# A decoder layer on one core: natural order in the first gate-and-up unit, sums placed behind the single block, two more weight sums made ahead

## The chip, the cores and the metric

The kernel runs on one core of a Trainium2 chip. The metric is the device time of one execution in microseconds (us), taken as the median of several runs; lower is better. The profile is of one execution of the same program.

## The reference

One decoder layer over 272 tokens (16 meta tokens in front of 256) of width 2048, in float32:

- s = s + 0.5 * FFN1(rms_norm(s)), where FFN(h) = (silu(h @ Wg) * (h @ Wu)) @ Wdown with a hidden width of 5632
- h = rms_norm(s); q, k, v, b, c, u = split(h @ w_in); a differential attention over q, k, v and a short gated convolution over b, c, u give two branches of width 1024
- each branch is multiplied by its w_branch, gated by sigmoid(h @ w_gate), and the two are added; s = s + merged @ w_out
- s = s + 0.5 * FFN2(rms_norm(s)), a last rms_norm, and the meta tokens are dropped

## The kernel before

Every matrix product is split into high and low parts: a tensor is cast to a high part (`wh` of the weights on ScalarE) and the rest is subtracted on VectorE (`wl`), and TensorE multiplies high by high, low by high and high by low. So each product of two blocks is three matmuls (lines 644 to 646 in the helper `product`).

The first FFN (`linear`, lines 360 to 439) multiplies plainly, weights stationary, 272 tokens wide. Most of what follows works on 256 tokens in `linear_mix` (line 622): a unit has an output of 2 x 512 columns (gate and up, or two gates) and runs over eight pairs of 128-row blocks of the weights. A pair is of one of three kinds, one letter each in a plan:

- D: the plain way, two tiles of two weight blocks, eight products, 24 matmuls of 128x512.
- S: Winograd's way with seven products, 21 matmuls. The weights are four tiles: a single block, two blocks, and two pairs of weight sums, t24 and t13. VectorE makes these sums on the spot in three operations (`sums`, lines 686 to 688).
- P: as S, but the weight sums were made ahead. In the first FFN a helper (`Making`, lines 316 to 339) loads quarters of such weights on POOL's DMA queue, VectorE adds them in three operations (lines 331 to 333), and POOL stores them to DRAM; `tick` starts a step of it every few chunks. A P pair loads three blocks and the two sums from there (lines 666, 673, 674), on the SP queue.

The activations have sums as well: `Mixed.sum_of_parts` (line 579) adds the parts of one pair, makes four sums of 128x128 blocks on VectorE (lines 589 to 592) and splits them (lines 614 and 615). Its temporaries carry the tag "sc", which has two buffers. The split of an S or P pair's single block takes two buffers of the same tag.

Products of one name are summed in one PSUM bank over the whole unit: D pairs feed 2, 3, 4 and x, S and P pairs feed 1 to 7. All eight banks are in use once a unit has seen both kinds, and x is complete with the last D pair; then `done` copies it out (line 736).

A unit's splits are issued ahead of its products: `step` holds the matmuls of up to three tiles back. Small work of other stages is spread through a unit by a list, `side`: one entry is taken when a pair's last tile is used. The entries of `out_done` (line 1234 on) turn the updated residual into the next operand h3: `turned(p)` transposes pair p on TensorE into a PSUM bank (line 1180), ScalarE and VectorE write its two parts (1184, 1185), and `sum_of_parts` follows. The order of the instructions on each engine comes from a scheduler that goes by this program order and by its own estimates of what is ready.

A plan holds the kinds, the pairs at which transposes of earlier results (`later`) are done, and a table that says behind which tile (pair, tile) which pair's weight sums are made. The plan of FFN2's first unit has a fifth entry, the order in which it goes through the pairs.

Of the kernel before, what the change touches and what calls it, by code (L numbers as in the profile page):

```python
# [15 lines left out]
P = 128  # L16
# [4 lines left out]
F = 5632  # L21
DC = D // P
GC = 4
GW = GC * P
# [17 lines left out]
LATER_AT = (4, 6)  # L42


GATES_FIRST = ("DDDSDSDS", (2,), {(2, 1): 3, (4, 1): 5, (6, 1): 7}, ())
GATES = ("PSDSDSDS", (), {(0, 3): 1, (2, 1): 3, (4, 1): 5, (6, 1): 7}, ())
Q = ("DSDSDSDS", (), {(0, 1): 1, (2, 1): 3, (4, 1): 5, (6, 1): 7}, ())
B_PLAN = ("DSDSDSDS", (2, 4), {(0, 1): 1, (2, 1): 3, (4, 1): 5, (6, 1): 7}, ())
FFN2_FIRST = ("DDPDPDPP", (1,), {}, (), (0, 1, 3, 4, 5, 2, 6, 7))
FFN2 = ("DDPPDSPP", (1,), {(4, 1): 5}, ())  # L50
FFN2_MORE = ("DPPPDSPP", (2,), {(4, 1): 5}, ())
OUT_FIRST = ("DDSDSDSD", (1,), {(1, 1): 2, (3, 1): 4, (5, 1): 6}, ())
OUT = ("DDDDSDSD", (), {(3, 1): 4, (5, 1): 6}, ())
DOWN_FIRST = ("DDDDSDSD", (1,), {(3, 1): 4, (5, 1): 6}, ())
DOWN = ("DDSDSDSD", (), {(1, 1): 2, (3, 1): 4, (5, 1): 6}, ())
DOWN_LAST = ("DDDSDS", (1,), {(2, 1): 3, (4, 1): 5}, ())
AHEAD = 3
W_LAST = 8 * GC
TICK_COUNT = 512
# [2 lines left out]
MORE_IN = (4, 5, 6, 7, 8, 9, 10)  # L62


def _made_in(plan):
    return [plan[4][i] if plan[4:] else i for i, kind in enumerate(plan[0]) if kind == "P"]


def _unit_plan(u):
    return FFN2_MORE if u in MORE_IN else FFN2 if u else FFN2_FIRST  # L70


GATE_UNITS = [GATES_FIRST] + [GATES] * (D // GW - 1)
MADE = [(0, d, p) for d, plan in enumerate(GATE_UNITS) for p in _made_in(plan)]
MADE += [(1, u, p) for u in range(F // GW) for p in _made_in(_unit_plan(u))]


@with_exitstack
def decoder_layer(ctx: ExitStack, tc: tile.TileContext, t, out):
    nc = tc.nc  # L80
# [5 lines left out]
    tmp = ctx.enter_context(tc.tile_pool(name="tmp", bufs=2))  # L86
# [46 lines left out]
    def load_vectors():  # L133
# [7 lines left out]
        out=mask[:, T - P :],  # L141
        in_=mask[:, T - P :],
# [152 lines left out]
    side = []  # L295
# [326 lines left out]
    def linear_mix(plan, a, w, name, done, k0=0, made=None, pairwise=False):  # L622

        kinds, turn_at, sums_at, by_load = plan[:4]
        at = plan[4] if plan[4:] else range(len(kinds))
        nd = kinds.count("D")
        ns = len(kinds) - nd
        left = {k: 2 * nd * (k in "234x") + ns * (k != "x") for k in "1234567x"}
        ps = {}

        def product(k, left_op, wh, wl):
            first = k not in ps
            if first:  # L640
                ps[k] = bank(name + k)
            left[k] -= 1
            hi, lo = left_op
            nc.tensor.matmul(ps[k], hi, wh, start=first, stop=False)  # L644
            nc.tensor.matmul(ps[k], lo, wh, start=False, stop=False)  # L645
            nc.tensor.matmul(ps[k], hi, wl, start=False, stop=left[k] == 0)  # L646
            if left[k] == 0:
                done(k, ps[k])

        def use(p, n, products):  # L650

            for k, left_op, wh, wl in products:
                product(k, left_op, wh, wl)
            if p in turn_at and later:
                later.pop(0)()
            if n == (1 if kinds[p] == "D" else 3):
                if p == 0:
                    flush()
                if side:
                    side.pop(0)()  # L660

        def load(p):

            st = wpool.tile([P, 4, GW], F32, tag="st", bufs=ST_BUFS, name="st")
            n = 3 if p in by_load or kinds[p] == "P" else 4
            nc.sync.dma_start(out=st[:, :n, :], in_=w[k0 // 2 + at[p], :, :n, :])
            if kinds[p] == "P":
                if pairwise:
                    t13s[p] = wpool.tile([P, 2, GW], F32, tag="tt", bufs=2, name="t13")
                else:  # L670
                    t13s[p] = aux.tile([P, 2, GW], F32, tag="act", name="t13")
                t24s[p] = wpool.tile([P, 2, GW], F32, tag="tt", bufs=2, name="t24")
                nc.sync.dma_start(out=t24s[p], in_=made[at[p]][:, 2:4, :])
                nc.sync.dma_start(out=t13s[p], in_=made[at[p]][:, 0:2, :])
            if kinds[p] == "S":
                if not by_load and (made is None or pairwise):
                    t13s[p] = wpool.tile([P, 2, GW], F32, tag="tt", bufs=2, name="t13")
                elif p not in by_load:
                    t13s[p] = aux.tile([P, 2, GW], F32, tag="act", name="t13")
                t24s[p] = wpool.tile([P, 2, GW], F32, tag="tt", bufs=2, name="t24")  # L680
            return st

        def sums(k):
            st, t13, t24 = loaded[k], t13s[k], t24s[k]
            if k not in by_load:
                nc.vector.tensor_add(t13, st[:, 1:3, :], st[:, 3:4, :].to_broadcast([P, 2, GW]))
            nc.vector.tensor_add(t24[:, 0, :], t13[:, 0, :], st[:, 2, :])
            last_sum[:] = [nc.vector.tensor_add(t24[:, 1, :], t24[:, 0, :], st[:, 0, :]).ins]  # L688

        t13s, t24s = {}, {}  # L690

        def prefetch(p):
            t13 = t13s[p] = aux.tile([P, 2, GW], F32, tag="act", name="t13")
            nc.gpsimd.dma_start(out=t13, in_=w[k0 // 2 + p, :, 1:3, :])
            nc.gpsimd.dma_start(out=t13, in_=w[k0 // 2 + p, :, 3:5, :], accum_op=ALU.add)

        far = 2 if by_load or (made is not None and not pairwise) else 1
        loaded = {k: load(k) for k in range(far)}
        for p, kind in enumerate(kinds):
            for k in by_load:  # L700
                if k == p + 4 or (p == 0 and k < 4):
                    prefetch(k)
            st = loaded[p]
            (a11, a21), (a12, a22) = ([a.block(2 * at[p] + c, i) for i in range(2)] for c in range(2))
            if kind == "D":
                tiles = [
                    (st[:, 1 - c :: 2, :], (("2", a1, 0), ("3", a1, 1), ("4", a2, 0), ("x", a2, 1)))
                    for c, (a1, a2) in enumerate(((a11, a21), (a12, a22)))
                ]
            else:  # L710
                s1, s2, s3, s4 = a.sums[at[p]]
                tiles = [
                    (st[:, 2:3, :], (("3", s4, 0),)),
                    (st[:, 0:2, :], (("1", a11, 1), ("2", a12, 0))),
                    (t24s[p], (("6", s2, 0), ("4", a22, 1))),
                    (t13s[p], (("5", s1, 0), ("7", s3, 1))),
                ]
            for n, (src, products) in enumerate(tiles):
                if n == 1 and p + far < len(kinds):
                    loaded[p + far] = load(p + far)  # L720
                wh, wl = parts(src, src.shape[1])
                if (p, n) in sums_at:

                    with tc.issue_after(part_last[1]):
                        sums(sums_at[p, n])
                products = [(k, left_op, wh[:, j, :], wl[:, j, :]) for k, left_op, j in products]
                step(lambda p=p, n=n, products=products: use(p, n, products), src.shape[1] > 1)
# [388 lines left out]
    for d in range(D // GW):  # L1116
# [28 lines left out]
        if d < 2:  # L1145
            n = 3 * d
# [93 lines left out]
    def out_done(u):  # L1240
        def f():
            if u == 0:
                side.append(lambda: None)
                for p in (0, 2):
                    side.append(lambda p=p: [turned(p), turned(p + 1), squares(0, 0, p // 2), squares(1, 0, p // 2)])
                side.append(lambda: [hn.sum_of_parts(2, tmp), hn.sum_of_parts(3)])
            else:
                side.extend(
                    (
                        lambda: [turned(4), squares(0, 1, 0), squares(1, 1, 0)],  # L1250
                        lambda: [turned(5), hn.sum_of_parts(5)],
                        lambda: [turned(6), squares(0, 1, 1), hn.sum_of_parts(6)],
                        lambda: [turned(7), squares(1, 1, 1)],
                        lambda: hn.sum_of_parts(7),
                        norm_tok,
                    )
                )

        return f
# [40 lines left out]
    for half in thirds:  # L1300
# [11 lines left out]
        for u in range(2):  # L1312
# [40 lines left out]
                )  # L1353
            elif u == 0:
                side.extend([lambda: None] * 2)
                side.extend(lambda p=p: ma.sum_of_parts(p) for p in (4, 6, 2))
                add_mix(DOWN_FIRST, ma, w_down, half[0] * GC, u, 0.5, "dma", lambda: None)
            elif not final:
                if half is thirds[0]:
# [90 lines left out]
```

## Time and profile before

| What | us |
|---|---|
| median of three runs | 2133.9 |
| lowest and highest of them | 2133.49 and 2135.06 |
| the profiled execution | 2133.6 |
| its span, first to last instruction | 2131.8 |
| TensorE busy | 2118.6 |
| VectorE busy | 1765.0 |
| ScalarE busy | 1138.7 |

The granted clock of TensorE is 0.999 of full speed over the span. Busy time is the union of an engine's instructions; matmuls overlap one another in the profile, so two of them that start 0.23 us apart each show 0.39 us. The stages follow one another as: first FFN (to some 770 us), k, q, b, v, c and u (to 1090), gates and branches (to 1350), out (to 1435), second FFN (to the end).

### The profile page before, as it was taken

Reading aid. Unit: us, or ns where it says so; the run is one execution under the profiler, and the core shown is the slowest. Engines: PE = TensorE matmul, PEld = TensorE weight load, DVE = VectorE, ACT = ScalarE, POOL = GpSimd, SP = SyncE. Lnnn points to the kernel's source line nnn. Section 1 sums busy time; section 2 is a strip of 40 time slices with the busy share of each in tenths; the row PEclk is TensorE's granted clock in tenths of the full one; section 3 lists DMA queues with packets and bytes.
Section 4 is the critical chain, followed back from the end, with each engine's and each line's share of the span. In section 5 each row is a group of like instructions: output and inputs, shape, how many; then the busy total and the mean of one; then the engine's idle time right before and its main releaser. Section 6 shows DMA issues by size and latency. Waiting matters only on the chain.

```text
span 2131.8 us, 33535 instructions
## 1 busy us (share of the span) xinstructions
PE 2118.6 (99%) x13096; PEld 1910.3 (90%) x13096; DVE 1765.0 (83%) x2458; ACT 1138.7 (53%) x1447; POOL 152.0 (7%) x241
## 2 busy tenths in 40 slices
PE   9999999999999999999999999999999999999998
PEld 9999999999999998899998888887888888888887
DVE  8777776677767878967888889998999999998997
ACT  6433343344443455645546655557665567656765
POOL 0111111111111110000000000000000100000000
PEclk9999999999999999999999999999999999999999
DMA  8989999999899875544455665566875988769863
GB/s 305 340 310 339 344 331 331 334 331 331 328 331 338 302 293 193 182 166 151 144 187 199 212 231 179 208 215 231 289 274 191 284 323 316 247 222 325 320 232 138
DMA packets 107007, 562.04 MB, mean 264 GB/s; under 512 B 12512, under 2 KB 12896, under 8 KB 66144
## 3 DMA queue, kind: packets, MB, share of 16 engines
q1 hardware_dynamic: 72720, 440.73, 57.6%
q0 software_dynamic: 33696, 118.50, 16.1%
q8 instruction: 102, 1.67, 0.3%
q10 hardware_dynamic: 432, 0.67, 0.1%
q14 instruction: 57, 0.47, 0.1%
HBM read 496.94 MB, written 58.72 MB: 261 GB/s over the span
## 4 chain that ended last, share of the span: by engine, by line
PE 99%; ACT 0%; DMA 0%; DVE 0%; issue 0%; SPq 0%; ACTq 0%
PE pg L644 6%; PE pg L645 6%; PE pg L646 6%; PE pd L427 4%; PE pd L425 4%; PE pu L425 4%; PE pu L426 4%; PE pu L427 4%; PE pd L426 4%; PE pg L425 4%; PE pg L427 4%; PE pg L426 4%; PE pd L644 4%; PE pd L646 4%; PE pd L645 4%; PE g L644 2%
## 5 line engine op out<-in xcount | busy, mean ns | idle before, releaser
L409 ACT CAST wh<-st 128x1024 fp32r<-128x1024 f32 x320 | 335.1, 1049 | 475.7 <-PE pu L426 143.2
L414 DVE TENSOR_TENSOR wl<-st,wh 128x1024 fp32r<-128x1024 f32 x320 | 390.3, 1223 | 217.9 <-ACT wh L409 217.7
L532 DVE TENSOR_TENSOR wl<-st,wh 128x1024 fp32r<-128x1024 f32 (+1 forms) x424 | 454.3, 1089 | 32.9 <-ACT wh L531 29.2
L531 ACT CAST wh<-st 128x1024 fp32r<-128x1024 f32 (+1 forms) x424 | 386.4, 945 | 153.6 <-PE pdx L645 27.7
L531 ACT CAST wh<-t 128x1024 fp32r<-128x1024 f32 x208 | 214.6, 1052 | 244.5 <-DVE t L688 184.0
L532 DVE TENSOR_TENSOR wl<-t,wh 128x1024 fp32r<-128x1024 f32 x208 | 248.2, 1221 | 58.8 <-ACT wh L531 54.4
L427 PE MATMUL pd<-mh,wl 128*128 128x272 f32 x704 | 203.1, 288 | 0.0
L425 PE MATMUL pg<-h,wh 128*128 128x272 f32 x704 | 201.9, 287 | 0.4 <-ACT wh L409 0.4
L425 PE MATMUL pd<-mh,wh 128*128 128x272 f32 x704 | 202.2, 287 | 0.0
L425 PE MATMUL pu<-h,wh 128*128 128x272 f32 x704 | 201.9, 287 | 0.0
L427 PE MATMUL pu<-h,wl 128*128 128x272 f32 x704 | 201.7, 287 | 0.0
L426 PE MATMUL pu<-h,wh 128*128 128x272 f32 x704 | 201.7, 286 | 0.0
L426 PE MATMUL pg<-h,wh 128*128 128x272 f32 x704 | 201.6, 287 | 0.0
L427 PE MATMUL pg<-h,wl 128*128 128x272 f32 x704 | 200.9, 287 | 0.0
L426 PE MATMUL pd<-ml,wh 128*128 128x272 f32 x704 | 200.8, 285 | 0.0
L645 PE MATMUL pg<-wh,h 128*128 128x512 f32 x373 | 146.1, 392 | 0.0
L644 PE MATMUL pg<-wh,h 128*128 128x512 f32 x373 | 145.5, 391 | 0.6 <-ACT h L1184 0.6
L646 PE MATMUL pg<-wl,h 128*128 128x512 f32 x373 | 145.4, 391 | 0.6 <-DVE wl L532 0.6
L426 PEld LDWEIGHTS pd<-ml,wh 128*128 128x128 f32 x704 | 133.5, 190 | 0.0
L425 PEld LDWEIGHTS pg<-h,wh 128*128 128x128 f32 x704 | 132.9, 189 | 0.7 <-ACT wh L409 0.7
L426 PEld LDWEIGHTS pg<-h,wh 128*128 128x128 f32 x704 | 132.8, 189 | 0.0
L426 PEld LDWEIGHTS pu<-h,wh 128*128 128x128 f32 x704 | 132.6, 188 | 0.0
(392 smaller groups left out, 5040.0 us busy)
## 6 DMA issues: line engine op xcount, KB each, us to landing
st<-in_ffn_w_gu_dram SPq DMA_DIRECT2D x121, 1024.0 KB, 7.4
st<-in_ffn_w_down_dram SPq DMA_DIRECT2D x82, 1024.0 KB, 7.1
mk<-in_ffn_made_of_dram POOLq DMA_DIRECT2D x108, 512.0 KB, 8.6
made<-mk POOLq DMA_DIRECT2D x108, 512.0 KB, 6.7
t<-made SPq DMA_DIRECT2D x108, 512.0 KB, 5.7
st<-in_ffn_w_gu_dram SPq DMA_DIRECT2D x51, 768.0 KB, 5.8
st<-in_w_in_dram SPq DMA_DIRECT2D x32, 1024.0 KB, 4.8
st<-in_w_gate_dram SPq DMA_DIRECT2D x29, 1024.0 KB, 4.8
```

The lines of the kernel that those rows point to most:

```text
L409: nc.scalar.copy(out=wh[:, :m, :], in_=sw)
L414: last_wl[:] = [nc.vector.tensor_sub(wl[:, :m, :], sw, wh[:, :m, :].bitcast(F32)).ins]
L425: nc.tensor.matmul(a, wh[:, i, f], act.part(c, 0, t0, t1), start=first, stop=False)
L426: nc.tensor.matmul(a, wh[:, i, f], act.part(c, 1, t0, t1), start=False, stop=False)
L427: nc.tensor.matmul(a, wl[:, i, f], act.part(c, 0, t0, t1), start=False, stop=last)
L531: part_last[:] = [nc.scalar.copy(out=wh, in_=src).ins]
L532: part_last.append(nc.vector.tensor_sub(wl, src, wh.bitcast(F32)).ins)
L644: nc.tensor.matmul(ps[k], hi, wh, start=first, stop=False)
L645: nc.tensor.matmul(ps[k], lo, wh, start=False, stop=False)
L646: nc.tensor.matmul(ps[k], hi, wl, start=False, stop=left[k] == 0)
```

## The change

1. FFN2's first unit goes through its pairs in natural order: D D D P D P P P over pairs 0 to 7, where it was pairs 0, 1, 3, 4, 5, 2, 6, 7 as D D P D P D P P. The kind of each pair stays. The code for such an order is removed.
2. In all plans the weight sums of an S pair are made behind the split of its own single block (place p, tile 0) and no longer behind the second tile of the plain pair before it (place p - 1, tile 1).
3. Two activation sums move in `side`: `hn.sum_of_parts(3)` three entries later in OUT's second unit, `ma.sum_of_parts(2)` two entries later in DOWN_FIRST.
4. In the first gate unit, places 1 and 3 become P pairs: D P D P D S D S for D D D S D S D S. The list of sums to be made ahead, MADE, grows from 54 to 56 pairs, and its makings (two halves a pair) from 108 to 112.

```diff
-GATES_FIRST = ("DDDSDSDS", (2,), {(2, 1): 3, (4, 1): 5, (6, 1): 7}, ())
-GATES = ("PSDSDSDS", (), {(0, 3): 1, (2, 1): 3, (4, 1): 5, (6, 1): 7}, ())
-Q = ("DSDSDSDS", (), {(0, 1): 1, (2, 1): 3, (4, 1): 5, (6, 1): 7}, ())
...
-FFN2_FIRST = ("DDPDPDPP", (1,), {}, (), (0, 1, 3, 4, 5, 2, 6, 7))
-FFN2 = ("DDPPDSPP", (1,), {(4, 1): 5}, ())
...
-OUT = ("DDDDSDSD", (), {(3, 1): 4, (5, 1): 6}, ())
+GATES_FIRST = ("DPDPDSDS", (2,), {(5, 0): 5, (7, 0): 7}, ())
+GATES = ("PSDSDSDS", (), {(0, 3): 1, (3, 0): 3, (5, 0): 5, (7, 0): 7}, ())
+Q = ("DSDSDSDS", (), {(1, 0): 1, (3, 0): 3, (5, 0): 5, (7, 0): 7}, ())
...
+FFN2_FIRST = ("DDDPDPPP", (1,), {}, ())
+FFN2 = ("DDPPDSPP", (1,), {(5, 0): 5}, ())
...
+OUT = ("DDDDSDSD", (), {(4, 0): 4, (6, 0): 6}, ())
...
-                side.append(lambda: [hn.sum_of_parts(2, tmp), hn.sum_of_parts(3)])
+                side.append(lambda: hn.sum_of_parts(2, tmp))
+                side.extend([lambda: None] * 2)
+                side.append(lambda: hn.sum_of_parts(3))
...
-                side.extend(lambda p=p: ma.sum_of_parts(p) for p in (4, 6, 2))
+                side.extend(lambda p=p: ma.sum_of_parts(p) for p in (4, 6))
+                side.extend([lambda: None] * 2)
+                side.append(lambda ma=ma: ma.sum_of_parts(2))
```

## Rows read from the trace of the kernel before

**Rows 1.** The page's first part: busy us, share of the span, instructions.
```profile
PE 2118.6 (99%) x13096; PEld 1910.3 (90%) x13096; DVE 1765.0 (83%) x2458; ACT 1138.7 (53%) x1447; POOL 152.0 (7%) x241
```

**Rows 2.** Windows: stretch, length, busy us (records) PE, PEld, DVE, ACT, POOL; clock; DMA share, GB/s.
```profile
50.00:750.00 700.00, 700.00 (x5668) 700.00 (x5667) 506.82 (x743) 282.45 (x318) 128.17 (x205) 1.00 0.90 330
...
1092.00:1142.00 50.00, 50.00 (x225) 41.37 (x224) 46.57 (x66) 31.05 (x40) 0.00 (x0) 1.00 0.57 194
...
1415.00:1435.00 20.00, 19.83 (x88) 16.07 (x87) 19.82 (x31) 10.36 (x13) 0.00 (x0) 1.00 0.59 198
1435.00:1460.00 25.00, 25.00 (x112) 19.80 (x111) 23.18 (x37) 18.05 (x29) 0.00 (x0) 1.00 0.77 270
1460.00:1486.00 26.00, 23.32 (x99) 16.76 (x98) 19.69 (x31) 17.12 (x22) 0.00 (x0) 1.00 0.62 211
1486.00:1506.00 20.00, 20.00 (x93) 16.60 (x93) 20.00 (x24) 13.38 (x16) 0.00 (x0) 1.00 0.72 257
1500.00:1526.00 26.00, 26.00 (x117) 21.52 (x116) 24.47 (x26) 18.77 (x22) 0.00 (x0) 1.00 0.84 286
```

**Rows 3.** Timeline of TensorE in the gates: start us, duration us, what.
```profile
1180.48 0.39 PE L644 MATMUL g<-wh,h 128*128 128x512 f32 x1
...
1181.16 0.39 PE L644 MATMUL g<-wh,h 128*128 128x512 f32 x1
```

**Rows 4.** Timeline of FFN2's first unit, its last three pairs.
```profile
1467.78 0.39 PE L646 MATMUL pgx<-wl,h 128*128 128x512 f32 x1
...
1468.92 0.58 ACT L736 COPY u2x<-pgx 128x512 f32<-128x512 f32 x1
...
1469.56 0.66 PE L1180 MATMUL h_ps<-ident,sT 128*128 128x128 f32 x4 [1.39 <-ACT u2x L736]
...
1475.27 0.63 ACT L531 CAST wh<-st 128x512 fp32r<-128x512 f32 x1
...
1476.66 0.68 DVE L532 TENSOR_TENSOR wl<-st,wh 128x512 fp32r<-128x512 f32 x1
...
1483.12 0.69 DVE L615 TENSOR_TENSOR sp<-sums,sp 128x512 fp32r<-128x512 f32 x1
```

**Rows 5.** Timeline of the first DOWN_FIRST at its second S pair.
```profile
1639.54 0.61 ACT L531 CAST wh<-st 128x512 fp32r<-128x512 f32 x1
1639.69 0.39 PE L645 MATMUL pd<-wh,m 128*128 128x512 f32 x1
...
1640.20 0.50 PE L644 MATMUL pd<-wh,sp 128*128 128x512 f32 x1
```

**Rows 6.** Timeline of a later gate unit at an S pair.
```profile
1244.10 0.69 DVE L532 TENSOR_TENSOR wl<-st,wh 128x512 fp32r<-128x512 f32 x1
...
1246.44 0.69 DVE L688 TENSOR_TENSOR t<-t,st 128x512 f32<-128x512 f32 x1
...
1248.32 2.36 DVE L532 TENSOR_TENSOR wl<-t,wh 128x1024 fp32r<-128x1024 f32 x2 [1.19 <-ACT wh L531]
...
1249.70 0.39 PE L646 MATMUL g<-wl,sp 128*128 128x512 f32 x1
```

**Rows 7.** VectorE's groups by line and shape: busy us, mean ns, idle before.
```profile
L532 DVE TENSOR_TENSOR wl<-st,wh 128x1024 fp32r<-128x1024 f32 x320 | 387.7, 1220 | 32.6 <-ACT wh L531 29.0 <-PE h_ps L1180 1.4
...
L331 DVE TENSOR_TENSOR mk<-mk 128x512 f32<-128x512 f32 x108 | 73.9, 685 | 0.9 <-DMA mk<-in_ffn_made_of_dram 0.9
L532 DVE TENSOR_TENSOR wl<-st,wh 128x512 fp32r<-128x512 f32 x104 | 71.2, 685 | 0.3 <-ACT wh L531 0.2
L686 DVE TENSOR_TENSOR t<-st 128x1024 f32<-128x1024 f32 x50 | 60.9, 1218 | 0.0
L333 DVE TENSOR_TENSOR mk<-mk 128x256 f32<-128x256 f32 x108 | 45.8, 424 | 3.0
```

**Rows 8.** DMA issues (KB, median us to landing); who ended ScalarE's idle time before L409.
```profile
t<-made SPq DMA_DIRECT2D x108, 512.0 KB, 5.7
...
  PE pu L426: 138.7, 79
```

More of the change, by code (lines that the diff above doesn't have):

```diff
@@ L42 @@
 LATER_AT = (4, 6)
-GATES_FIRST = ("DDDSDSDS", (2,), {(2, 1): 3, (4, 1): 5, (6, 1): 7}, ())
-GATES = ("PSDSDSDS", (), {(0, 3): 1, (2, 1): 3, (4, 1): 5, (6, 1): 7}, ())
-Q = ("DSDSDSDS", (), {(0, 1): 1, (2, 1): 3, (4, 1): 5, (6, 1): 7}, ())
-B_PLAN = ("DSDSDSDS", (2, 4), {(0, 1): 1, (2, 1): 3, (4, 1): 5, (6, 1): 7}, ())
-FFN2_FIRST = ("DDPDPDPP", (1,), {}, (), (0, 1, 3, 4, 5, 2, 6, 7))
-FFN2 = ("DDPPDSPP", (1,), {(4, 1): 5}, ())
-FFN2_MORE = ("DPPPDSPP", (2,), {(4, 1): 5}, ())
-OUT_FIRST = ("DDSDSDSD", (1,), {(1, 1): 2, (3, 1): 4, (5, 1): 6}, ())
-OUT = ("DDDDSDSD", (), {(3, 1): 4, (5, 1): 6}, ())
-DOWN_FIRST = ("DDDDSDSD", (1,), {(3, 1): 4, (5, 1): 6}, ())
-DOWN = ("DDSDSDSD", (), {(1, 1): 2, (3, 1): 4, (5, 1): 6}, ())
-DOWN_LAST = ("DDDSDS", (1,), {(2, 1): 3, (4, 1): 5}, ())
+GATES_FIRST = ("DPDPDSDS", (2,), {(5, 0): 5, (7, 0): 7}, ())
+GATES = ("PSDSDSDS", (), {(0, 3): 1, (3, 0): 3, (5, 0): 5, (7, 0): 7}, ())
+Q = ("DSDSDSDS", (), {(1, 0): 1, (3, 0): 3, (5, 0): 5, (7, 0): 7}, ())
+B_PLAN = ("DSDSDSDS", (2, 4), {(1, 0): 1, (3, 0): 3, (5, 0): 5, (7, 0): 7}, ())
+FFN2_FIRST = ("DDDPDPPP", (1,), {}, ())
+FFN2 = ("DDPPDSPP", (1,), {(5, 0): 5}, ())
+FFN2_MORE = ("DPPPDSPP", (2,), {(5, 0): 5}, ())
+OUT_FIRST = ("DDSDSDSD", (1,), {(2, 0): 2, (4, 0): 4, (6, 0): 6}, ())
+OUT = ("DDDDSDSD", (), {(4, 0): 4, (6, 0): 6}, ())
+DOWN_FIRST = ("DDDDSDSD", (1,), {(4, 0): 4, (6, 0): 6}, ())
+DOWN = ("DDSDSDSD", (), {(2, 0): 2, (4, 0): 4, (6, 0): 6}, ())
+DOWN_LAST = ("DDDSDS", (1,), {(3, 0): 3, (5, 0): 5}, ())
 AHEAD = 3
@@ L62 @@
 MORE_IN = (4, 5, 6, 7, 8, 9, 10)
-def _made_in(plan):
-    return [plan[4][i] if plan[4:] else i for i, kind in enumerate(plan[0]) if kind == "P"]
 def _unit_plan(u):
@@ L73 @@
 GATE_UNITS = [GATES_FIRST] + [GATES] * (D // GW - 1)
-MADE = [(0, d, p) for d, plan in enumerate(GATE_UNITS) for p in _made_in(plan)]
-MADE += [(1, u, p) for u in range(F // GW) for p in _made_in(_unit_plan(u))]
+MADE = [(0, d, p) for d, plan in enumerate(GATE_UNITS) for p, kind in enumerate(plan[0]) if kind == "P"]
+MADE += [(1, u, p) for u in range(F // GW) for p, kind in enumerate(_unit_plan(u)[0]) if kind == "P"]
 @with_exitstack
@@ L622, in linear_mix @@
     def linear_mix(plan, a, w, name, done, k0=0, made=None, pairwise=False):
-        kinds, turn_at, sums_at, by_load = plan[:4]
-        at = plan[4] if plan[4:] else range(len(kinds))
+        kinds, turn_at, sums_at, by_load = plan
         nd = kinds.count("D")
@@ L665, in load @@
             n = 3 if p in by_load or kinds[p] == "P" else 4
-            nc.sync.dma_start(out=st[:, :n, :], in_=w[k0 // 2 + at[p], :, :n, :])
+            nc.sync.dma_start(out=st[:, :n, :], in_=w[k0 // 2 + p, :, :n, :])
             if kinds[p] == "P":
@@ L672, in load @@
                 t24s[p] = wpool.tile([P, 2, GW], F32, tag="tt", bufs=2, name="t24")
-                nc.sync.dma_start(out=t24s[p], in_=made[at[p]][:, 2:4, :])
-                nc.sync.dma_start(out=t13s[p], in_=made[at[p]][:, 0:2, :])
+                nc.sync.dma_start(out=t24s[p], in_=made[p][:, 2:4, :])
+                nc.sync.dma_start(out=t13s[p], in_=made[p][:, 0:2, :])
             if kinds[p] == "S":
@@ L703, in linear_mix @@
             st = loaded[p]
-            (a11, a21), (a12, a22) = ([a.block(2 * at[p] + c, i) for i in range(2)] for c in range(2))
+            (a11, a21), (a12, a22) = ([a.block(2 * p + c, i) for i in range(2)] for c in range(2))
             if kind == "D":
@@ L710, in linear_mix @@
             else:
-                s1, s2, s3, s4 = a.sums[at[p]]
+                s1, s2, s3, s4 = a.sums[p]
                 tiles = [
```

## The prediction

> **What bounds the kernel now.** I read the page first: TensorE is busy in 2118.6 of 2131.8 us [rows 1], so only two things can shorten the program: fewer matmuls, or matmuls that follow one another where today they don't. Then I cut the span into stretches. From 50 to 750 us TensorE is busy all the time, and so it is in the gates [rows 2]. The exception is the first unit of the second FFN. Its row of 1460 to 1486 us has 99 matmul records, where the same 26 us a unit later have 117; 8 of the 99 are small transposes. So 117 - 91 = 26 wide matmuls are missing. Two wide products of three matmuls start 0.68 us apart [rows 3], 0.227 us for a matmul, which makes 5.9 us; the two groups of four transposes took some 0.65 us each of it [rows 4]. About 4.6 us are lost here, and the profile's idle time (26.00 - 23.32) shows just over half of that.
>
> The timeline tells what is late [rows 4]. Eight products hold all eight PSUM banks until a unit's last plain ("D") pair ends the product x. The transposes `turned(6)` of this unit need a bank, so they sat behind x: its last matmul starts at 1467.78, ScalarE copies x out at 1468.92, the transposes start at 1469.56. Behind them stands a serial chain (ScalarE and VectorE write h3, `sum_of_parts(6)`, the split of its sums, then the cast of the next pair's single block at 1475.27 and its subtraction at 1476.66), over at 1477.34. That is 9.6 us from x to the single block's low part. Pair 6 is the very next pair, so TensorE has almost nothing else. A second chain of the same sort, for pair 7, ends with its sums' low part at 1483.81.
>
> Smaller losses: in the down units a matmul starts 0.51 us after the one before, at 1639.69 and 1640.20, where 0.23 is the pitch [rows 3, 5]. It needs the single block of an S pair, whose cast (1639.54) came late. The single block and `sum_of_parts` share the tag "sc" with two buffers, and two sums had been put ahead of it in program order. The pattern stands three times (OUT's second unit, both DOWN_FIRST), 0.3 us each.
>
> **The change, part by part.**
>
> *Natural order of the first unit.* The pairs and kinds are the same; pair 2 (plain) moves from place 5 to place 2, so x ends with pair 4 at place 4. Now `turned(4)`, `turned(5)` and `turned(6)` are all issued (after pairs 0, 1 and 2) before the first P pair takes the last banks. Only `turned(7)` waits for x, and pair 7 is at place 7. What is late next is therefore the chain of pair 7. By the order in which the code issues steps, three tiles behind the splits, `sum_of_parts(7)` comes ahead of pair 6's single block, so that block again stands behind a 9.6 us chain through "sc". But between x and it TensorE now has pair 5 (21 matmuls, 4.8 us), the transposes (0.65 us) and the 18 matmuls of pair 6 that don't need the block (4.1 us): 9.5 us. The chain is just covered if VectorE is as free as it was. It will be less free: it idled 6.3 of the 26 us in that window and not at all in the 20 us behind it [rows 2]. I take 1.1 us as left of the 4.6, between nothing and all of it, nearer to nothing because the cover almost equals the chain; 3.5 us come back. No queue carries more: the loads are the same, in another order, and three P pairs in a row load as MORE units do.
>
> *Sums moved.* `sum_of_parts(3)` goes from OUT's fourth step to its seventh, `sum_of_parts(2)` in DOWN_FIRST two steps back: now behind the S pair's single block. Each third of a microsecond above had this cause; 3 x 0.3 = 0.9 us, bounds 0 and 0.9. The sums are needed later still: pair 3 comes at place 3 of the next unit instead of 2, pair 2 in the next down unit.
>
> *First gate unit.* Place 1 turns from D (24 matmuls) to P (21): 3 x 0.227 = 0.68 us off TensorE. Place 3 turns from S to P, with the same matmuls. VectorE: D splits two blocks of 1.22 us, P one of 0.69 and three of 1.22, so place 1 adds 1.9 us; place 3 loses the three sum operations, 1.22 + 0.69 + 0.69 = 2.6 us [rows 7]. It nets to 0.7 us less, beside matmuls. SP issues three loads for each of the two pairs instead of one, 0.77 MB more each, in a stage with a DMA share of 0.57 [rows 2]. Pair 3's made sums must wait for pair 1's two "tt" buffers, and pair 4's load is queued behind them on SP. They come free at the latest when TensorE ends pair 1; then pair 2 and the first two tiles of pair 3 (24 and 9 matmuls, 7.5 us) stand ahead of the made sums, against 5.7 us for the load [rows 8] and 2.3 us for cast and subtraction. That is 0.5 us at worst; the splits run ahead of the matmuls, so I take 0. Without that cover the load would cost 5.7 us once.
>
> *Four more makings (two pairs, two halves) in the first FFN.* Each is 512 KB in and 512 KB out, 4.2 MB in all on POOL's queue, and 0.69 + 2 x 0.42 = 1.5 us of VectorE, 6 us together [rows 7]. VectorE is busy 507 of 700 us there, and ScalarE's casts waited for buffers that TensorE held, not for loads [rows 2, 8]; so 0. If DMA were the bound, 4.2 MB at the 330 GB/s of that stretch would be 12.7 us.
> The Trainium skill ("DMA: Bandwidth & Descriptors", Specifications) gives about 358 GB/s as the limit of one core's HBM traffic. By that the stretch, at 330 and then about 336, stays under it, and the sum stays as it is; but the margin is thin, so this speaks against the change.
>
> *Sums on the spot.* In all plans the three sum operations of an S pair stand behind the subtraction of its own single block, not behind the plain pair before. In the gates the order so far was L686, single block, L687, second block, L688 [rows 6]; the new one holds the same five operations, so L688 should end when it did. Then come the cast and a subtraction that ends at 1249.55, 0.15 us before the matmul that reads it (1249.70). I take 0. Below: nothing is gained by a block that is early, since TensorE didn't wait for it (0). Above: L688 ends 0.69 us later (the single block in front, nothing filled in behind), which is 0.54 us beyond the slack in each of the 19 S pairs of Q, B and the gates, 10.3 us.
>
> **Sum.** 3.5 + 0.9 + 0.7 = 5.1 us off the profiled execution's 2133.6 (span 2131.8 and 1.8 around it): 2128.5. The median of the runs is 0.3 above that execution: 2128.8.
>
> **Rivals.** *The chain of pair 7 still stalls.* Code order and "sc" speak for it, the 9.5 us of cover against it. With nothing recovered, 0.9 + 0.7 remain: 2132.3; with half of the 4.6, 2130.
>
> *VectorE is the bound of the stretch.* From 1415 to 1506 us it is busy 19.82 + 23.18 + 19.69 + 20.00 = 82.7 of 91 us [rows 2]. At the 93% of 1435 to 1460 that work takes 88.9 us: 2.1 us come back, and the time is 2133.9 - 2.1 - 1.6 = 2130.2. Against it: the 20 us behind ran at 100% without a stall.
>
> *The sums on the spot delay every S pair* (the other side): 2128.8 + 10.3 = 2139. It decides once L688 ends more than 0.15 us later against the matmuls. Against it: the same operations in sum.
>
> *The makings tip DMA over*: 2128.8 + 12.7 = 2141.5, from the point where the casts of the first FFN wait for loads; no such row stands now.
> The limit on that skill page is the rule by which this would come out; the trace so far, at 330 GB/s, stays below it.
>
> **How the numbers follow.** The forecast has 0.58, the pair-7 chain 0.20, VectorE as the bound 0.13, the sums 0.05, the makings 0.04. A change of 0.2% (4.3 us) is about what a measurement of this kernel can tell from none: faster means under 2129.6. The forecast is faster, the two middle rivals are the same, the last two slower: 0.58, 0.33, 0.09. The low end has all 4.6 us back, 2133.9 - 6.2 = 2127.7, and 0.7 for what the window of 1435 to 1460 us lost: it has 104 wide matmuls and 8 small ones where the rate of 1500 to 1526 us gives 112.5 wide ones [rows 2], 1.9 us less some 1.3 for the transposes. That makes 2127.0. The high end takes in the chain rival with 0.7 us of the sums' bound: 2133.0. The last two rivals stay outside.
>
> **What would show it.** Right: the window of the first unit's last three pairs loses its gap; `turned(7)` alone follows x; the single blocks in OUT and DOWN_FIRST come in time; 3 matmuls fewer in the first gate unit; no wait for loads in the first FFN. Wrong: waits of TensorE for VectorE's low parts at pair 6 or 7 or in the following unit, or many small gaps in Q, B and the gates.

## The result and the profile after

The changed kernel took 2137.95 us (median of 13 runs, 2137.11 to 2139.86); the kernel before, run beside it, 2134.77 (13 runs, 2133.34 to 2136.47). The ratio is 1.0016, 95% interval 1.0009 to 1.0023: slower by about 3.2 us. By the 0.2% that I had set this is a tie, to which I had given 0.33; but the interval lies above 1, and the time lies 5 us above my range of 2127.0 to 2133.0, towards the two rivals that I had given 0.09 together. I had forecast 5.1 us less; it became 3.2 more, so 8.3 us have to be accounted for. (The forecast of 2128.8 is 9.2 us below the result because the kernel before also came out 0.9 us above its earlier median.)

In the changed kernel, and in those built on it, line numbers are 4 or 5 lower: the casts and splits of the mixed units are L527 and L528 (were 531 and 532), the three weight sums L681 to L683 (686 to 688), a making's additions L327 to L329 (331 to 333), the matmuls L639 to L641 (644 to 646). Runs 2, 4 to 7 and 10 are built on the kernel before and have its numbers. The page's first part:

```profile
PE 2119.2 (99%) x13093; PEld 1909.4 (89%) x13093; DVE 1771.5 (83%) x2469; ACT 1136.5 (53%) x1449; POOL 157.3 (7%) x249
```

The three matmuls fewer are there (13096 in [rows 1]), the span is 2136.3 us, and the granted clock is 0.998, against 0.999 before. TensorE is idle for 17.1 us of its span, where it was for 13.2: the time went to waiting. What TensorE waited for, in total, times and longest:

```profile
PE pd L639 <- ACT wh L527: 2.6, 2, 1.6
PE pd L423 <- DVE wl L410: 1.8, 2, 1.1
PE pg L639 <- ACT wh L527: 1.4, 1, 1.4
...
PE b L639 <- ACT wh L527: 0.4, 1, 0.4
PE pd L641 <- DVE wl L528: 0.3, 1, 0.3
PE g L639 <- ACT wh L527: 0.2, 1, 0.2
```

None of these is the wait that the change went for (transposes behind x): that one is gone. There are new ones: for the high part of a weight sum in the down units, in b and in a gate; for a plain low part in the first FFN (L423); and one at the end of FFN2's first unit.

TensorE's timeline gives a ledger, the time of each stage. A stage runs from the first matmul into one set of banks to the first into the next. FFN2 goes through its hidden width in three thirds, each with its gate-and-up units and then its down units; the last down is that of the last third. Stages that an edit doesn't touch come out equal to 0.02 us in every kernel of this study up to 1090 us, and to 0.1 behind it, so that one profile of each kernel suffices for them. Three stages vary by themselves: the start-up (0.1 to 1.1 us longer in each kernel, with another wait for the first weights each time), the units of FFN2's first third (0.8 in the control, run 10) and the last down (-0.4 to 0.3 where its code is as before). Difference to the kernel before, us; the columns behind the first are the experiments below:

| stage | changed | run 1: old sums | run 4: order only | run 5: sums in gates | run 6: sums in downs | run 8: 480 ticks |
|---|---|---|---|---|---|---|
| start-up | 0.64 | 1.14 | 0.78 | 0.25 | 0.14 | 0.60 |
| first FFN, last down | 2.59 | 2.99 | 0.00 | 0.00 | 0.00 | 0.00 |
| b | 0.43 | -0.01 | 0.00 | 0.49 | 0.01 | 0.01 |
| first gate unit | -0.68 | -0.68 | 0.00 | 0.00 | 0.00 | -0.68 |
| other gates, branches | 1.02 | 0.01 | 0.00 | 1.08 | 0.02 | 0.10 |
| OUT | 0.23 | -0.47 | -0.47 | -0.47 | 0.22 | -0.47 |
| FFN2, first third's units | -2.56 | -3.32 | -3.21 | -4.26 | -4.07 | -3.84 |
| its down units | 1.79 | -0.37 | -0.41 | -0.37 | 1.91 | -0.37 |
| second third's units | 0.33 | -0.07 | -0.05 | -0.02 | 0.29 | -0.03 |
| its down units | -0.44 | -0.45 | -0.45 | -0.45 | -0.41 | -0.45 |
| last down | 1.20 | -0.34 | 0.31 | 0.32 | 2.06 | 0.08 |

The first column adds up to 4.6 us where the medians differ by 3.2: the profiled execution of the kernel before (2133.6) was faster than its median here (2134.77), that of the changed kernel (2138.09) was not.

Three readings of the changed kernel made the theories.

**The first FFN's last down.** VectorE, ScalarE, POOL's queue and TensorE there (start, duration, what, in brackets the idle time before and what ended it):

```profile
750.50 1.23 DVE L410 TENSOR_TENSOR wl<-st,wh 128x1024 fp32r<-128x1024 f32 x1 [1.75 <-ACT wh L405]
760.39 0.69 DVE L327 TENSOR_TENSOR mk<-mk 128x512 f32<-128x512 f32 x1 [8.67 <-DMA mk<-in_ffn_made_of_dram]
761.12 0.43 DVE L328 TENSOR_TENSOR mk<-mk 128x256 f32<-128x256 f32 x1
761.46 1.22 DVE L410 TENSOR_TENSOR wl<-st,wh 128x1024 fp32r<-128x1024 f32 x1
...
752.35 1.05 ACT L405 CAST wh<-st 128x1024 fp32r<-128x1024 f32 x1 [1.88 <-PE pd L422]
...
750.21 1.14 POOL L323 DMA_DIRECT2D mk<-in_ffn_made_of_dram  x2 [1.73 <-DMA made<-mk]
...
761.33 0.28 PE L422 MATMUL pd<-ml,wh 128*128 128x272 f32 x1
762.74 0.39 PE L423 MATMUL pd<-mh,wl 128*128 128x272 f32 x1 [1.12 <-DVE wl L410]
```

A making's load was issued only at 750.21, when the store of its buffer's last contents had landed, and itself landed as the addition started, 10 us later. VectorE stood at the addition for 8.67 us, and the split of the next weights (L410 at 761.46), which it had behind the addition, started only after it, though the cast that the split needs was done at 753.40. TensorE ran out of low parts at 761.33 and, as the delay was passed on, again at 772. In the kernel before the addition at this place starts without a wait:

```profile
756.91 0.69 DVE L331 TENSOR_TENSOR mk<-mk 128x512 f32<-128x512 f32 x1
```

**The second down unit of the first third.** VectorE, ScalarE and TensorE at its first S pair:

```profile
1656.16 0.68 DVE L1191 SCALAR_TENSOR_TENSOR sT<-pdx,sT 128x512 f32<-128x512 f32 x1
...
1656.76 0.68 DVE L579 TENSOR_TENSOR mf<-h 128x512 f32<-128x512 f32 x1
...
1660.62 0.89 DVE L594 TENSOR_TENSOR h<-sums,h 128x128 fp32r<-128x128 f32 x4
...
1660.94 0.62 ACT L527 CAST wh<-st 128x512 fp32r<-128x512 f32 x1
...
1661.61 0.69 DVE L528 TENSOR_TENSOR wl<-st,wh 128x512 fp32r<-128x512 f32 x1
...
1662.22 1.22 DVE L681 TENSOR_TENSOR t<-st 128x1024 f32<-128x1024 f32 x1
...
1663.48 0.69 DVE L682 TENSOR_TENSOR t<-t,st 128x512 f32<-128x512 f32 x1
1664.20 0.69 DVE L683 TENSOR_TENSOR t<-t,st 128x512 f32<-128x512 f32 x1
...
1665.00 2.00 ACT L527 CAST wh<-t 128x1024 fp32r<-128x1024 f32 x2 [3.44 <-DVE t L683]
...
1664.08 0.39 PE L641 MATMUL pd<-wl,m 128*128 128x512 f32 x1
1666.10 0.50 PE L639 MATMUL pd<-wh,sp 128*128 128x512 f32 x1 [1.63 <-ACT wh L527]
```

An activation sum (L579 to L594) takes both "sc" buffers; the single block's cast starts only when its additions are done, at 1660.94, and its subtraction when its split is done, at 1661.5; and the weight sums, now behind the single block, start at 1662.22 and end at 1664.89, when TensorE has already used up all that doesn't need them. VectorE at the same S pair in the kernel before:

```profile
1655.69 1.22 DVE L686 TENSOR_TENSOR t<-st 128x1024 f32<-128x1024 f32 x1
...
1657.84 0.68 DVE L687 TENSOR_TENSOR t<-t,st 128x512 f32<-128x512 f32 x1
1658.44 0.68 DVE L532 TENSOR_TENSOR wl<-st,wh 128x512 fp32r<-128x512 f32 x1
1659.04 0.68 DVE L688 TENSOR_TENSOR t<-t,st 128x512 f32<-128x512 f32 x1
```

Two of the three weight sums stand ahead of the single block there, within the wait for "sc". L688 ends 53.2 us after the stage's first matmul; in the changed kernel L683, the same sum, ends 56.7 us after it, 3.5 us later.

**The end of FFN2's first unit.** ScalarE's first cast of the next unit, and the matmul that needs it:

```profile
1489.17 3.57 ACT L527 CAST wh<-st 128x1024 fp32r<-128x1024 f32 x4 [1.62 <-DMA st<-in_ffn_w_gu_dram]
...
1490.27 0.50 PE L639 MATMUL pg<-wh,h 128*128 128x512 f32 x1 [1.38 <-ACT wh L527]
```

The gap around x is gone, but the next unit's weights come late. The windows show the shift:

```profile
1460.00:1486.00 26.00, 25.89 (x114) 20.39 (x113) 25.50 (x45) 19.33 (x25) 0.00 (x0) 1.00 0.67 229
1486.00:1506.00 20.00, 18.62 (x86) 15.14 (x85) 18.02 (x22) 14.29 (x17) 0.00 (x0) 1.00 0.75 262
```

The first window has 114 records where [rows 2] has 99, with VectorE busy for 25.50 of its 26 us; the second lost 7 of its 93, to the wait for a load. What the issue of that load waited for, on VectorE and on SP's queue:

```profile
1481.85 1.82 DVE L528 TENSOR_TENSOR wl<-st,wh 128x512 fp32r<-128x512 f32 x2
...
1482.56 12.14 SPq L661 DMA_DIRECT2D st<-in_ffn_w_gu_dram  x5
```

The first of the two subtractions, that of a single block, ends at 1482.53, and the load is issued at 1482.56: it had waited for a weight buffer, and this subtraction released it.

### The profile page after: what moved, and what is told of

Read it like the earlier page. It is cut to its first block, busy times and chain, and to the rows that moved or that the text cites. A ratio compares the mean times of both kernels' runs of the same rounds, so it can differ in the third digit from the quotient of the medians.

```text
span 2136.3 us, 33571 instructions
## 1 busy us (share of the span) xinstructions
PE 2119.2 (99%) x13093; PEld 1909.4 (89%) x13093; DVE 1771.5 (83%) x2469; ACT 1136.5 (53%) x1449; POOL 157.3 (7%) x249
## 4 chain that ended last, share of the span: by engine, by line
PE 90%; DVE 6%; issue 2%; DMA 1%; ACT 1%; SPq 0%; ACTq 0%; DVEq 0%
PE pg L639 6%; PE pg L641 6%; PE pg L640 6%; PE pu L422 4%; PE pu L423 4%; PE pu L421 4%; PE pg L423 4%; PE pg L422 4%; PE pg L421 4%; PE pd L423 3%; PE pd L421 3%; PE pd L422 3%; PE pd L639 3%; PE pd L641 3%; PE pd L640 3%; DVE wl L528 2%
## 5 line engine op out<-in xcount | busy, mean ns | idle before, releaser
L410 DVE TENSOR_TENSOR wl<-st,wh 128x1024 fp32r<-128x1024 f32 x320 | 390.1, 1223 | 206.3 <-ACT wh L405 206.2
L528 DVE TENSOR_TENSOR wl<-st,wh 128x1024 fp32r<-128x1024 f32 (+1 forms) x424 | 450.3, 1086 | 26.6 <-ACT wh L527 21.5
L527 ACT CAST wh<-st 128x1024 fp32r<-128x1024 f32 (+1 forms) x424 | 383.9, 943 | 130.6 <-PE pdx L640 32.0
L527 ACT CAST wh<-t 128x1024 fp32r<-128x1024 f32 x210 | 216.2, 1052 | 244.8 <-DVE t L683 158.8
L528 DVE TENSOR_TENSOR wl<-t,wh 128x1024 fp32r<-128x1024 f32 x210 | 249.9, 1221 | 64.9 <-ACT wh L527 61.4
L423 PE MATMUL pd<-mh,wl 128*128 128x272 f32 x704 | 203.4, 289 | 1.8 <-DVE wl L410 1.8
L423 PE MATMUL pu<-h,wl 128*128 128x272 f32 x704 | 201.7, 287 | 0.0
L423 PE MATMUL pg<-h,wl 128*128 128x272 f32 x704 | 200.9, 287 | 0.0
L639 PE MATMUL pg<-wh,h 128*128 128x512 f32 x373 | 145.6, 390 | 1.4 <-ACT wh L527 1.4
L641 PE MATMUL pg<-wl,h 128*128 128x512 f32 x373 | 145.7, 392 | 0.0
L423 PEld LDWEIGHTS pd<-mh,wl 128*128 128x128 f32 x704 | 132.2, 188 | 2.5 <-DVE wl L410 2.5
```

The lines of the kernel that those rows point to most:

```text
L410: last_wl[:] = [nc.vector.tensor_sub(wl[:, :m, :], sw, wh[:, :m, :].bitcast(F32)).ins]
L423: nc.tensor.matmul(a, wl[:, i, f], act.part(c, 0, t0, t1), start=False, stop=last)
L527: part_last[:] = [nc.scalar.copy(out=wh, in_=src).ins]
L528: part_last.append(nc.vector.tensor_sub(wl, src, wh.bitcast(F32)).ins)
```

## The experiments

Ten kernels ran, each beside the kernel before on the same chip (2134.5 to 2134.8 us there). Theory A: the sums on the spot cost several us. Theory B: the additional makings cost 2.6 in the first FFN. Rival C: neither, the scheduler's order merely fell otherwise. One profile was taken of each kernel.

**1. The changed kernel with the weight sums where they were** (behind the plain pair before).

```diff
-Q = ("DSDSDSDS", (), {(1, 0): 1, (3, 0): 3, (5, 0): 5, (7, 0): 7}, ())
+Q = ("DSDSDSDS", (), {(0, 1): 1, (2, 1): 3, (4, 1): 5, (6, 1): 7}, ())
...
```


> The changed kernel with the weight sums of S pairs back behind the plain pair before them; all else as changed. Theory A (the sums on the spot are late in the S pairs: stages b +0.4, gates and branches +1.0, OUT's lost 0.3 gain, the first down +1.8 where the moved sum alone would give -0.3, the last down +1.2, some 5 us in all): about 5 us under the changed kernel, 2.0 to 2.5 us under the kernel before, and those stages last as they did before. Theory B (the makings' new pace is what costs, 2.6 us in the last down stage of the first FFN): no more than 1 us under the changed kernel; the stall near 760 us stays under both theories. Rival C (any change of the program order reshuffles the scheduler's order and costs by chance): stalls stay, at other places.

2130.78 us (2129.12 to 2132.53), ratio 0.9982 [0.9973, 0.9991]. So the sums cost 2137.95 - 2130.78 = 7.2 us within the change.

**2. The kernel before with only the sums on the spot.**

```diff
-DOWN = ("DDSDSDSD", (), {(1, 1): 2, (3, 1): 4, (5, 1): 6}, ())
+DOWN = ("DDSDSDSD", (), {(2, 0): 2, (4, 0): 4, (6, 0): 6}, ())
...
```


> The kernel before with the sums on the spot alone. Theory A: about 5 us slower than before (2138 to 2140), in b, gates, the first down stage and the last one. Theory B: the same as before within 1 us. Rival C: slower or faster by a different amount than the difference of the changed kernel and its twin with the old sums.

2144.28 us (2141.84 to 2144.91), ratio 1.0042 [1.0028, 1.0055]: 9.5 us by themselves, more than within the change. In the ledger OUT loses 2.13 and the second third's downs 1.49 here, against a loss of 0.23 and a gain of 0.44 within the change, where two activation sums stand behind the S pair's single block. A holds, larger than I had put it. That the sums cost another amount here than within the change is also what rival C expected; these two stages alone make up for the difference (2.13 here against 0.70 from run 1 to the changed kernel, and 1.49 against 0.01), so what the sums cost depends on the order around them.

**3. The changed kernel with the first gate unit as before** (54 pairs made ahead).

```diff
-GATES_FIRST = ("DPDPDSDS", (2,), {(5, 0): 5, (7, 0): 7}, ())
+GATES_FIRST = ("DDDSDSDS", (2,), {(3, 0): 3, (5, 0): 5, (7, 0): 7}, ())
```


> The changed kernel with the first gate unit as before (108 makings, not 112), sums on the spot kept. Theory B: the last down stage of the first FFN takes 119.1 us again instead of 121.7, the first gate unit 0.7 longer; 1.9 us under the changed kernel. Theory A alone: 0.7 us over the changed kernel. Should the first FFN's loss come from the DMA load as such, it goes too, but then the stages before 670 us would have lost as well.

2135.12 us (2134.15 to 2136.40), ratio 1.0003 [0.9994, 1.0011]: 2.8 us less than the changed kernel. The ledger has 0.00 in the first FFN's last down, and no stall at 761. B holds: the edit that takes 0.68 us off TensorE costs 2.6 elsewhere. These two make 1.9 of the 2.8 us; most of the rest lies in the units of FFN2's first third (-3.70 here, -2.56 in the changed kernel), which vary by themselves.

**4. The kernel before with only the natural order and the moved activation sums.**

```diff
-FFN2_FIRST = ("DDPDPDPP", (1,), {}, (), (0, 1, 3, 4, 5, 2, 6, 7))
+FFN2_FIRST = ("DDDPDPPP", (1,), {}, ())
...
-                side.append(lambda: [hn.sum_of_parts(2, tmp), hn.sum_of_parts(3)])
+                side.append(lambda: hn.sum_of_parts(2, tmp))
+                side.extend([lambda: None] * 2)
+                side.append(lambda: hn.sum_of_parts(3))
...
```


> The kernel before with the natural order of FFN2's first unit and the two moved activation sums, nothing else. Both theories: about 3.5 us under the kernel before (2.6 from the unit, 0.9 from the small stalls of OUT and DOWN_FIRST): 2131. If the small stalls are not due to the sums in front of the single block: 2.6 alone. If the order gains more without the sums on the spot (the gap of 1.4 us behind the unit in the changed kernel is theirs): up to 4.6 + 0.9.

2128.92 us (2128.26 to 2130.08), ratio 0.9973 [0.9962, 0.9984]: 5.8 us faster. From here to the changed kernel it is 1.9 for the gate edit with its makings (2130.78 - 2128.92, run 1) and 7.2 for the sums; that these make the 3.2 measured is so by construction, as each step starts where the one before it ended. What speaks against C are repeats: the gate edit costs 1.9 and, with the sums on the spot, 2.8 (run 3); the sums cost 7.2 and, without the gate edit, 6.2 (2135.12 - 2128.92, runs 3 and 4); and the ledger has the losses in the same stages each time. So C doesn't explain the loss. Its part is what separates 7.2 from the 9.5 of run 2, and about 1 us elsewhere.

**5 and 6. Where do the sums cost?** Run 4 with the sums on the spot only in Q, B and the gates, and only in OUT, FFN2's units and its downs.

```diff
 # 5
-Q = ("DSDSDSDS", (), {(0, 1): 1, (2, 1): 3, (4, 1): 5, (6, 1): 7}, ())
+Q = ("DSDSDSDS", (), {(1, 0): 1, (3, 0): 3, (5, 0): 5, (7, 0): 7}, ())
...
 # 6
-DOWN = ("DDSDSDSD", (), {(1, 1): 2, (3, 1): 4, (5, 1): 6}, ())
+DOWN = ("DDSDSDSD", (), {(2, 0): 2, (4, 0): 4, (6, 0): 6}, ())
...
```


> The kernel of before with natural order and moved activation sums (2128.9 us), and the weight sums on the spot behind the single block only in Q, B and the gates. Theory (the loss of the sums sits where the pair's activation sums and the results' additions share VectorE and the two sc buffers, in OUT and the second FFN's last products; in Q, B and the gates it is only the end of the chain that comes some tenths later): b +0.4, four gate and branch stages +0.2 to +0.4 each, together about +1.5, so 2130.4. Rival (the bound of my prediction: 0.5 us at each of the 19 S pairs of Q, B and the gates): +7 to +10, so 2136 to 2139.

2130.66 us (2129.84 to 2134.04), ratio 0.9983 [0.9974, 0.9992]: 1.7 us over run 4, where the theory had 1.5 and the bound of my prediction 7 to 10.

> As the run before, but the weight sums on the spot only in OUT, the second FFN's units and its down units. Theory: here lies most of the loss, OUT +0.7 to +2.6, first unit of the second FFN about +0.7, two downs +2.2 each, last down +1.5: +6 to +8, so 2135 to 2137, with stalls of 1 to 2 us before a low-part matmul of the second S pair of each down. Rival: under +1, so at most 2130, since these are few S pairs.

2134.20 us (2133.37 to 2136.97), ratio 1.0000 [0.9991, 1.0009]: 5.3 over run 4, somewhat under the theory's 6 to 8. The two add up to 7.0, against the 7.2 and 6.2 above. VectorE and TensorE in the down unit of run 6:

```profile
1651.69 0.69 DVE L583 TENSOR_TENSOR mf<-h 128x512 f32<-128x512 f32 x1
...
1655.37 0.90 DVE L598 TENSOR_TENSOR h<-sums,h 128x128 fp32r<-128x128 f32 x4
1656.37 0.69 DVE L532 TENSOR_TENSOR wl<-st,wh 128x512 fp32r<-128x512 f32 x1
1656.98 1.22 DVE L686 TENSOR_TENSOR t<-st 128x1024 f32<-128x1024 f32 x1
...
1658.96 0.69 DVE L688 TENSOR_TENSOR t<-t,st 128x512 f32<-128x512 f32 x1
...
1660.85 0.50 PE L644 MATMUL pd<-wh,sp 128*128 128x512 f32 x1 [1.52 <-ACT wh L531]
```

The same picture as in the changed kernel: activation sum, then the single block, then three weight sums in a row, then 1.52 us of waiting.

**7. Is it the activation sum in front?** Run 6 with that one activation sum two entries later.

```diff
-                    side.extend((lambda: None, lambda: hn.sum_of_parts(1, h3)))
+                    side.extend([lambda: None] * 3 + [lambda: hn.sum_of_parts(1, h3)])
```


> The run with the sums on the spot in OUT, the second FFN and its downs (2134.2 us), and in the first third's second down unit the activation sum of pair 1 two entries later, so that it no longer stands in front of the first S pair's single block. Theory (the single block waits for the two sc buffers that this activation sum holds until 1656.3, and the weight sums now stand behind the single block): the 1.7 us stall at 1659 goes, this down stage falls from 1.9 above that of before to between 0.4 below and 0.3 above, 2132.0 to 2132.5; the last down keeps its 2 us. Rival (three sums in a row are late by themselves, whatever stands in front of the single block): the stall stays over 1 us, 2134.

2134.28 us (2133.36 to 2138.19), ratio 1.0000 [0.9991, 1.0009]: no gain in the median over run 6 (2134.20), so the expected 2132 was missed. VectorE at the same S pair, and TensorE at the next one:

```profile
1652.38 1.81 DVE L532 TENSOR_TENSOR wl<-st,wh 128x1024 fp32r<-128x1024 f32 x2
1654.12 1.22 DVE L686 TENSOR_TENSOR t<-st 128x1024 f32<-128x1024 f32 x1
...
1657.11 0.69 DVE L688 TENSOR_TENSOR t<-t,st 128x512 f32<-128x512 f32 x1
1658.45 0.69 DVE L583 TENSOR_TENSOR mf<-h 128x512 f32<-128x512 f32 x1 [0.65 <-PE pd L645]
...
1670.77 0.50 PE L644 MATMUL pd<-wh,sp 128*128 128x512 f32 x1 [0.37 <-ACT wh L531]
```

Without the activation sum in front, L688 ends at 1657.80 instead of 1659.65 (54.2 instead of 56.8 us after the stage's first matmul), and TensorE doesn't wait there. So what stands in front was the cause of the 1.52 us at this place. But the sum now stands in front of the next S pair's single block (0.37 us at 1670), and a wait of 0.2 us comes up in a unit behind it: in the ledger the down stage falls from 1.91 to 0.87, and the second third's units rise from 0.29 to 0.79. Half of the 1.0 us gained is passed on in this way; that the median shows nothing of the rest stays open, the more so as this profile (2133.36) is the fastest execution of the run. Theory right at the place, not in the time. OUT and the last down lose 0.69 and 1.75 us from run 4 to run 6. There VectorE's rows in run 6 show the same order, an activation sum (from 1372.25 and 2073.82), the single block, then the first weight sum (1378.47 and 2080.98), and TensorE waits behind it (0.34 us at 1383.61, 0.94 at 2086.71), but no run tested it. A tag of its own for the single block was not tried.

**8 and 9. Load or wait?** Run 1 with the makings spread over 480 ticks, and run 1 with the addition four steps behind its load.

```diff
 # 8
-TICK_COUNT = 512
+TICK_COUNT = 480
 # 9
-MAKE_AHEAD = 3
+MAKE_AHEAD = 4
```


> The changed kernel with the weight sums where they were (2130.8 us) and the makings spread over 480 ticks in place of 512, so that they end some 45 us before the end of the first FFN. Theory (one making's add stood on VectorE for its load at 752 to 760 us, beside the loads for the last chunks, and 2.6 us went there): the two stalls at 761 and 772 are gone and the last down stage of the first FFN is as before: 2128.2. Rival (four more makings cost their DMA time wherever they stand, and a quicker pace adds to it): stalls at other places in the first FFN, 2131 or more.

2127.72 us (2127.38 to 2129.00), ratio 0.9968 [0.9955, 0.9980].

> The changed kernel with the weight sums where they were (2130.8 us) and each making's add four steps behind its load in place of three, over the same 512 ticks. Theory (the add waits for its load, nothing else): a step of 6 us more covers most of the 8.7 us wait; the stall at 761 shrinks under 0.5 and 1.5 to 2.6 us come back: 2128.2 to 2129.3. Rival (five buffers: with four steps ahead each load waits for the store of the buffer's last tenant on POOL's queue, so that it starts later by as much): no gain, 2130.8 or more, with POOL waiting for stores.

2128.08 us (2127.30 to 2128.89), ratio 0.9970 [0.9959, 0.9981]. Each gives back some 3 us (3.1 and 2.7), with all 112 makings done. POOL's queue in run 9:

```profile
756.35 0.54 POOL L323 DMA_DIRECT2D mk<-in_ffn_made_of_dram  x1 [7.92 <-DMA made<-mk]
...
766.13 0.55 POOL L323 DMA_DIRECT2D mk<-in_ffn_made_of_dram  x1 [7.76 <-DMA made<-mk]
```

Run 8's group of a making's first addition (busy us, mean ns, idle before):

```profile
L327 DVE TENSOR_TENSOR mk<-mk 128x512 f32<-128x512 f32 x112 | 76.7, 685 | 0.0
```

The throughput of run 8 in 40 slices, from its page:

```profile
GB/s 299 363 331 356 356 346 345 353 341 354 336 349 360 296 179 192 199 178 141 157 188 196 230 212 182 208 230 239 284 277 193 283 323 316 249 226 322 320 230 139
```

Rival of run 9 half right: the loads do wait 7.9 us on POOL's queue for the store of their buffer, but nobody waits for them any more. In run 8 no addition waits for its load (0.0, where it was 8.7 in the changed kernel), although up to 363 GB/s move in the first FFN, more than in any slice of the changed kernel (347). So DMA throughput was not the cause; one addition's place in VectorE's order was. These two are the fastest kernels of the study, 10 us ahead of the changed one and 1 us ahead of run 4.

**10. Control: the kernel before over 480 ticks.**

```diff
-TICK_COUNT = 512
+TICK_COUNT = 480
```


> The kernel of before with its 108 makings over 480 ticks in place of 512: a control for the run in which the same pace change gave back 3 us. Theory (the 2.6 us were one making's wait at the end of the first FFN, which the kernel of before does not have): no change, 2134.4 to 2135.0, the last down stage of the first FFN within 0.1 us. Rival (the makings of before cost time there too, or the later pace is better in itself): 2 us or more faster; or slower, if a quicker pace costs by itself.

2134.44 us (2133.43 to 2135.42), ratio 1.0000 [0.9991, 1.0009], 0.00 in the last down of the first FFN. The pace is worth nothing by itself; it removes one collision.

**The end of the first unit across runs.** Of the kernels in natural order, the changed one and runs 1 and 4 have a stall there (1.4, 1.0 and 1.0 us); runs 3 and 5 to 9 have none. ScalarE's first casts of the next unit in run 4:

```profile
1484.50 3.66 ACT L531 CAST wh<-st 128x1024 fp32r<-128x1024 f32 x4 [1.24 <-DMA st<-in_ffn_w_gu_dram]
```

The same in run 5:

```profile
1484.24 1.98 ACT L531 CAST wh<-st 128x1024 fp32r<-128x1024 f32 x2
```

The DMA issues of 1477 to 1484 us in run 4 (size, median us to landing):

```profile
st<-in_ffn_w_gu_dram SPq DMA_DIRECT2D x1, 1024.0 KB, 6.2
```

The same in run 5:

```profile
st<-in_ffn_w_gu_dram SPq DMA_DIRECT2D x1, 1024.0 KB, 4.8
```

The load is issued late in both, at 1478.27 and 1479.35, as soon as VectorE is done with a single block. Where it lands in 4.6 to 4.9 us TensorE doesn't wait for it and the stage gives back 3.5 to 4.3 us; where it takes 6.2 to 6.5, in the changed kernel and runs 1 and 4, it gives back 2.6 to 3.3. Why it lands sooner in one profile than in another stays open: the instructions of this stretch are the same in runs 1, 8 and 9, of which only run 1 stalls, and one profile of each can't tell a kernel's habit from an execution's.

## Why the prediction was wrong

**Sums on the spot: taken as 0, cost 7.2 us.** This is the step that failed first: "the new one holds the same five operations, so L688 should end when it did". I read it in a gate unit [rows 6], where it nearly holds: there and in b runs 4 and 5 differ by 1.6 us in the ledger, far from the upper bound of 10.3. I did not read it in OUT and the second FFN, and 5.3 us lie there, most of it in OUT and the downs. There the same operations don't start at the same time. The old place let VectorE add weight sums while the single block waited for "sc"; the new one puts them behind that wait, and in front of the single block stands an activation sum. Run 7 shows this for one S pair of a down unit; for OUT and the last down it is read from the same order, not tested. The facts were in the prediction, which had "sc" as the cause of the late single blocks [rows 5], and let this edit hang three more operations on it. The rival for these sums gave 2139, close to the result, but through the gates; as a mechanism it was not this one, and that its number came close is luck.

**Makings: taken as 0, cost 2.6 to 3.0.** The step was that ScalarE's casts wait for buffers and not for loads. True, and also in the changed kernel no cast of the first FFN waited for its weights after the first 50 us. But the makings' own additions wait for loads, in VectorE's order, with the weight splits behind them. [Rows 7] had the sign, an idle time of 0.9 us before L331 that a load ended. My bound asked only what the bytes cost.
The Trainium skill ("Perfetto Trace Analysis", Roofline) calls the 358 GB/s that I had weighed a share for two active cores, and says that one core alone can pull more. Run 8's slices of 360 and 363 GB/s, and 376 GB/s from 55 to 85 us, without a wait of an addition, agree; I had weighed the wrong rule.

**Natural order: 3.5 forecast, 2.6 measured in the changed kernel, 3.2 to 4.3 elsewhere.** The mechanism was right: the wait of the transposes for x is gone, and of the pair-7 chain 0.2 to 0.4 us of waiting on its sums are left in most runs. What I overlooked is where else that chain ends: a single block that is split late also releases a weight buffer late, and the next unit's first load waits for that. "No queue carries more" holds for the bytes, but where that load then takes 6.2 us or more to land it costs 1.0 to 1.4.

**Sums moved: 0.9 forecast, 1.3 measured** (0.47, 0.37 and 0.45, the three stages of run 8): the mechanism was right, the size a little small.

**First gate unit: 0.68 forecast, 0.68 measured.** The 0.5 us of risk in its made sums did not come.

**VectorE as the bound of 1415 to 1506:** not seen where no load is late, as more than its 2.1 us came back there. In the changed kernel, which got 2.6, it is not excluded as a part: VectorE is busy for 25.50 of 26 us ahead of 1486, and one of its splits frees the buffer of the late load.

The sum, in medians: 7.2 for the sums on the spot and 2.5 for the makings (1.9 lost by the gate edit where 0.7 was to be gained), both taken as nothing, less 1.4 by which order and moved sums came out better in run 4 (5.8 for 4.4), make the 8.3 us between forecast and result, as they must by the way the runs follow from one another.

## What to carry to other kernels

When an instruction is moved, ask what the instruction that it now follows waits for, and read that at every place where the pattern stands, not at one. Work with no wait of its own is best put ahead of work that waits for a shared buffer; behind it, it inherits the wait. For added background work, bytes over bandwidth are only half of the price: look for the in-order engine on which it waits for its own transfer, and give it a longer lead or end it earlier.

## What the hardware showed unexpectedly

Two 128x512 additions on VectorE that follow one another and depend on each other start 0.72 us apart (1663.48 and 1664.20 above), where an addition and an independent operation of the same size, as at 1656.16 and 1656.76, start 0.60 apart. The last two of three weight sums in a row pay that; with a split between them, as in the kernel before (1657.84, 1658.44, 1659.04), each starts 0.60 after the one before.

Up to 1090 us, stages that an edit left alone took the same time to 0.02 us in twelve kernels, the start-up excepted. There a difference of 0.4 us could be told from a single profile, far under what the medians tell.
